# Attention on one Trainium2 core: the four weighted-sum rows of a head pair in one run behind the last transposes

## The chip, the cores and the metric

The kernel runs on one core of one Trainium2 chip. The metric is the device time of one execution in microseconds (us); the host only lays data out before the launch. The kernel is written by hand on top of a scheduler that decides the order of instructions where the code does not pin it; TensorE (PE) does matmuls and transposes, VectorE (DVE) and ScalarE (ACT) do elementwise work, GpSimd (POOL) and SyncE (SP) issue the DMAs here.

## The reference

The model is a two-layer trunk over 512 positions of width 1024. Layer 0 mixes positions with stick-breaking attention, layer 1 with a state-space layer; each is followed by a gated feed-forward block. The change is in layer 0's attention, of which this is the core (16 heads of 64, four blocks of 128 query positions):

```python
z = jnp.einsum('bhqd,bhkd->bhqk', q_blk, kf) * scale
mask = key_pos[None, :] < q_pos[:, None]
log_beta = jax.nn.log_sigmoid(z)
log_1mb = jnp.where(mask, jax.nn.log_sigmoid(-z), 0.0)
suffix = lax.cumsum(log_1mb, axis=3, reverse=True) - log_1mb
w = jnp.where(mask, jnp.exp(log_beta + suffix), 0.0)
o = jnp.einsum('bhqk,bhkd->bhqd', w, vf)
```

The weight of a key is its beta times the product of (1 - beta) over the keys between it and the query. That product telescopes: with R the running product of (1 - beta) from the right, the weight is a difference of two neighbouring values of R, so the kernel multiplies R by differences of V rows and needs no exponentials.

## The kernel before, in words

Heads are worked in eight pairs (pr = 0 to 7; h2 is the head in the pair). For a pair there are, in this order:

- **Projections** (`proj`): q and k of both heads as 128x512 tiles. Numbers are split in a high and a low part, so each product is three matmuls (`mm3`, lines L171, L174, L175). 8 products make k, then 8 make q. ACT and DVE evict them (L770 to L774).
- **Scores** (`z_row`, L782): row i of four, 128 queries against the first (i+1)*128 keys (at least 256), four matmuls (L792, L793). ACT makes `om = sigmoid(-z)` (L797), DVE runs a multiplying scan over it from the right (L798). The om tiles are full 128x512 tiles from one pool of nine (`OMB`).
- **Transposes** (`t_grp`, L803): group 0 turns column block 0 of the four rows, group 1 block 1 of three rows, group 2 blocks 2 and 3; so 8, 6 and 6 transposes for the two heads (L810). ACT evicts each head's group to a `wT` tile (L813), from a pool of four (`NWT`).
- **Weighted sums** (`av`, L818): for row j of the transposed weights and each head, one matmul of 64 output columns (L826) that adds into the pair's `o` bank: 512, 384, 256 and 128 columns for j = 0 to 3. The two heads use the two halves of the array. ACT evicts the sum (L832, or L828 and L829 for pairs 6 and 7).

The order on PE is written by hand (`tc.keep_in_program_order`, here `pe_pin`). `middle(pr)` (L864) serves pairs 1 to 6: it puts the projections of pair pr+1 in pieces between the scores of pair pr and the transposes and sums of pair pr-1. In `follow` order, ACT's and DVE's instructions stay in the written order as well. Into DVE's queue it also puts the `work` steps: up to four multiplications per pair of a weight row block `wg` with the conditioning vector (L198), whose 512 KB are loaded by a DMA that POOL issues (L197) into one of two buffers. `window(7)` and `window(8)` (L836) do the same for the last pairs, with products of the output projection `wo` as the filling; behind them `out_proj` ends the attention.

PSUM has eight banks: six in the pool `mm` and two in `aux`. Row tiles of the scores go to the one or the other (`ZM`), transposes to `mm`, and for pair 7 to `aux` (`TAUX`).

Before the change, `middle` has the sums of rows 0 and 1 ahead of transpose group 2, and the sums of rows 2 and 3 ahead of the scores of row 3.

Of the kernel before, what the change touches and what calls it, by code (L numbers as in the profile page):

```python
# [7 lines left out]
F32 = mybir.dt.float32  # L8
# [3 lines left out]
AF = mybir.ActivationFunctionType  # L12
ALU = mybir.AluOpType
# [3 lines left out]
P = 128  # L17
T = 512
# [40 lines left out]
NU = 4  # L59
NPRE = 3  # L60
KPRE = 5
NWT = 4
MIDN = 2
TAIL = 3
QK = 'kq'
BGA = 3
ZM = ((1, 0), (1, 1), (3, 0), (3, 1))
OMB = 9
TAUX = 7

_COLS = [("c0", KD), ("norm_mix", 2 * KD), ("norm_ffn", 2 * KD), ("b_mod", 96), ("norm_out", KD),
# [18 lines left out]
def _trunk(ctx, tc, I, out, tap):  # L90
    nc = tc.nc
    V, S, G, PE, SP = nc.vector, nc.scalar, nc.gpsimd, nc.tensor, nc.sync
# [13 lines left out]
    def bank(p=None, name="ps"):  # L106
        p = p or mm
        return p.tile([P, 512], F32, tag="b", name=name)
# [22 lines left out]
    maskb = cp.tile([P, T], BF16, tag="maskb", name="maskb")  # L131
# [5 lines left out]
    pin = {"head": []}  # L137
# [112 lines left out]
    def pe_pin(ins):  # L250
        tc.keep_in_program_order(ins)
# [290 lines left out]
    def attention(acc):  # L542
        with ExitStack() as av_, ExitStack() as ac:
# [168 lines left out]
            ap = ac.enter_context(tc.tile_pool(name="attn", bufs=1, reuse_waits="tile"))  # L712
# [20 lines left out]
            scale = HD ** -0.5  # L733
# [12 lines left out]
            def proj(pr, todo=None):  # L746
                units, r = [], [None, None]
                qk[pr] = r
                order = free if todo is None else follow

                def unit(s, w, ps, k):
                    mm3(ps, wk(w, k), (h[0][k], h[1][k]), k == 0, k == KD - 1, pr > 0)
                    if k == KD - 1:
                        if todo is None:
                            evict(s, ps)
                        else:
                            todo.append(lambda: evict(s, ps))

                def evict(s, ps):

                    lo, hi = slice(0, HD), slice(HD, P)
                    if s:
                        kl = kz[pr % 2]
                        st = [ap.tile([P, T], F32R, tag=g, bufs=2, name=f"{g}{pr}") for g in ("kA", "kB")]
                    else:
                        st = [np_.tile([P, T], F32, tag=g, bufs=2, name=f"q_{g}{pr}").bitcast(F32R) for g in ("sq", "nt1")]

                    heads = ((st[0], lo, hi), (st[1], hi, lo))
                    for t, own, other in heads:
                        order("S", lambda: S.activation(t[own], ps[own], AF.Copy))  # L770
                        if s:
                            order("S", lambda: S.activation(t[other], ps[own], AF.Copy))
                    for h2, (t, own, other) in enumerate(heads):
                        order("V", lambda: V.tensor_tensor(kl[h2][own] if s else t[other], ps[own], t[own].bitcast(F32), ALU.subtract))  # L774
                    r[s] = st + kl if s else st

                for nm in QK:
                    s, w, ps = "qk".index(nm), qkw[pr, nm], bank(name=f"{nm}{pr}")
                    units += [lambda s=s, w=w, ps=ps, k=k: unit(s, w, ps, k) for k in range(KD)]
                return units  # L780

            def z_row(pr, i, order=free):  # L782
                qs, ks = qk[pr]
                if i == 0:
                    wts[pr] = [[None] * 4 for _ in range(2)]
                n = (i + 1) * P
                m = max(n, 2 * P)
                zs = []
                for h2 in range(2):
                    z = bank(mm if (i, h2) in ZM else aux, f"z{pr}_{i}_{h2}")  # L790
                    q = qs[h2][:, i * P:(i + 1) * P]
                    pe_pin(PE.matmul(z[:, :m], q, ks[h2][:, :m], start=True, stop=False))  # L792
                    pe_pin(PE.matmul(z[:, :m], q, ks[2 + h2][:, :m], start=False, stop=True))  # L793
                    zs.append(z)
                for h2 in range(2):
                    om = ap.tile([P, T], F32, tag="om", bufs=OMB, name="om")
                    order("S", lambda: S.activation(om[:, :n], zs[h2][:, :n], AF.Sigmoid, scale=-scale))  # L797
                    pin["scan"] = order("V", lambda: V.tensor_tensor_scan(om[:, :n][:, ::-1], om[:, :n][:, ::-1], maskb[:, T - n:][:, ::-1], 1.0, ALU.mult, ALU.max))  # L798
                    wts[pr][h2][i] = om

            wT = {}
# [1 line left out]
            def t_grp(pr, gi, order=free):  # L803
                js = ((0,), (1,), (2, 3))[gi]
                for h2 in range(2):
                    pt = bank(aux if pr >= TAUX else mm, name=f"t{pr}_{h2}_{gi}")
                    c = 0
                    for j in js:
                        for i in range(j, 4):
                            pe_pin(PE.transpose(pt[:, c:c + P], wts[pr][h2][i][:, j * P:(j + 1) * P], ident))  # L810
                            c += P
                    t = ap.tile([P, T], F32, tag="wT", bufs=NWT, name="wT")
                    order("S", lambda: S.activation(t[:, :c], pt[:, :c], AF.Identity, bias=ones[:, 0:1], scale=-1.0))  # L813
                    wT[pr, h2, gi] = t
# [3 lines left out]
            def av(pr, js, order=free):  # L818
                if 0 in js:
                    po[pr] = bank(name=f"o{pr}")  # L820
                for j in js:
                    for h2 in range(2):
                        src = wT[pr, h2, min(j, 2)]
                        src = src[:, 256:384] if j == 3 else src[:, :T - j * P]
                        hd = (2 * pr + h2) * HD
                        pe_pin(PE.matmul(po[pr][h2 * HD:(h2 + 1) * HD, j * P:], vn[:, j, hd:hd + HD], src, start=j == 0, stop=j == 3))  # L826
                if 3 in js and pr >= 6:
                    S.activation(oh[pr], po[pr], AF.Copy)  # L828
                    V.tensor_tensor(ol[pr], po[pr], oh[pr].bitcast(F32), ALU.subtract)  # L829
                elif 3 in js:  # L830
                    o = otile(pr, f"oT{pr}")
                    order("S", lambda: S.activation(o, po[pr], AF.Copy))  # L832
                    tap(f"o{pr}", o)
                    oT[pr] = o

            def window(pr, units, fill=FILL, hooks={}):  # L836
                n, done = len(units), 0
                pv = pr - 1
                for st, share in enumerate(fill):
                    want = -(-n * share // 16)  # L840
                    for u in units[done:want]:
                        u()
                    done = max(done, want)
                    if pv >= 0:
                        if st == TST[0]:
                            t_grp(pv, 0)
                            t_grp(pv, 1)
                        if st == TST[1]:
                            av(pv, (0, 1))
                            t_grp(pv, 2)  # L850
                        if st == TST[2]:
                            av(pv, (2, 3))
                    if pr < 8 and st < 4:
                        z_row(pr, st)
                    if st in hooks:
                        hooks[st]()
                for u in units[done:]:
                    u()
# [5 lines left out]
            def middle(pr, gemvs, split, own=lambda k: None):  # L864
                todo, pv = [], pr - 1
                units = proj(pr + 1, todo)
                work = lambda q: bg(gemvs[q], lined=True, queue=G)

                def run(a, b):
                    for u in units[a:b]:  # L870
                        u()

                run(0, 7)
                work(0)
                split[0]()
                work(1)
                t_grp(pv, 0, follow)
                t_grp(pv, 1, follow)
                z_row(pr, 0, follow)
                run(7, 8)  # L880
                z_row(pr, 1, follow)
                work(2)
                todo[0]()
                split[1]()
                run(8, 13)
                own(0)
                av(pv, (0, 1), follow)
                t_grp(pv, 2, follow)
                z_row(pr, 2, follow)
                own(1)  # L890
                run(13, 16)
                todo[1]()
                av(pv, (2, 3), follow)
                z_row(pr, 3, follow)
                for k in range(2, KPRE):
                    own(k)
# [742 lines left out]
```

## Time and profile before

| what | value |
|---|---|
| time, median of 3 runs | 1176.8 us (1173.6 to 1178.79) |
| span of the profiled execution | 1174.0 us |
| PE busy | 1158.9 us, 99% |
| DVE busy | 857.7 us, 73% |
| ACT busy | 563.5 us, 48% |
| attention's weighted sums on PE | first at 101.0 us, last at 237.7 us of the span |

The span runs from the first to the last instruction of one profiled execution; no time of its own is given for that execution beside its span. It is 2.8 us under the median of the three timed runs, and inside their spread. In the profile a matmul's end is modelled and matmuls overlap, so what a piece of PE work costs is read from the starts of rows that follow each other, not from the second column of a row. A row of the timeline gives start, length, engine, line, operation, the tiles written and read, shape and count; a bracket gives idle time ahead of it and what ended it.

### The profile page before, as it was taken

Reading aid. Unit: us, or ns where it says so; the run is one execution under the profiler, and the core shown is the slowest. Engines: PE = TensorE matmul, PEld = TensorE weight load, DVE = VectorE, ACT = ScalarE, POOL = GpSimd, SP = SyncE. Lnnn points to the kernel's source line nnn. Section 1 sums busy time; section 2 is a strip of 40 time slices with the busy share of each in tenths; the row PEclk is TensorE's granted clock in tenths of the full one; section 3 lists DMA queues with packets and bytes.
Section 4 is the critical chain, followed back from the end, with each engine's and each line's share of the span. In section 5 each row is a group of like instructions: output and inputs, shape, how many; then the busy total and the mean of one; then the engine's idle time right before and its main releaser. Section 6 shows DMA issues by size and latency. Waiting matters only on the chain.

```text
span 1174.0 us, 16592 instructions
## 1 busy us (share of the span) xinstructions
PE 1158.9 (99%) x6242; PEld 964.2 (82%) x6242; DVE 857.7 (73%) x1311; ACT 563.5 (48%) x896; POOL 270.8 (23%) x278
## 2 busy tenths in 40 slices
PE   8999999999999999999999999999999999999997
PEld 7887777699788888888889888789888888888887
DVE  6968888775998666787757599887598378744555
ACT  6756667456453244413346477647443144422443
POOL 2001110000298799979800000000000000000003
PEclk8999999999999999999999999999999999999999
DMA  8873656331267858797756598671176357432322
GB/s 320 292 264 116 192 162 195 111 123 55 78 189 268 247 167 252 198 292 253 230 151 223 149 353 293 207 255 50 49 231 217 107 153 184 133 123 73 92 69 72
DMA packets 91618, 211.01 MB, mean 180 GB/s; under 512 B 19601, under 2 KB 37905, under 8 KB 91538
## 3 DMA queue, kind: packets, MB, share of 16 engines
q1 hardware_dynamic: 78562, 191.08, 51.0%
q0 software_dynamic: 4656, 16.78, 4.5%
q10 hardware_dynamic: 8320, 2.10, 0.8%
q8 instruction: 49, 0.80, 0.3%
q14 instruction: 31, 0.25, 0.1%
HBM read 188.68 MB, written 21.24 MB: 179 GB/s over the span
## 4 chain that ended last, share of the span: by engine, by line
PE 78%; DVE 7%; issue 7%; DMA 5%; ACT 2%; POOL 1%; SPq 1%; POOLq 0%; DVEq 0%; ACTq 0%
PE up L171 13%; PE up L174 13%; PE up L175 13%; PE dn L171 6%; PE dn L174 6%; PE dn L175 6%; DMA wg<-in_w_modT_dram 3%; PE u L174 1%; PE u L171 1%; PE u L175 1%; PE wo L171 1%; PE wos L174 1%; PE wo L175 1%; PE wo L174 1%; PE wos L175 1%
## 5 line engine op out<-in xcount | busy, mean ns | idle before, releaser
L171 PE MATMUL up<-hH,up_h 128*128 128x512 f32 x640 | 249.7, 391 | 0.3 <-DVE ca L461 0.3
L175 PE MATMUL up<-hH,up_l 128*128 128x512 f32 x640 | 249.3, 390 | 0.3 <-DVE up_l L166 0.3
L174 PE MATMUL up<-hL,up_h 128*128 128x512 f32 x640 | 249.3, 390 | 0.0
L461 DVE SCALAR_TENSOR_TENSOR ca<-up,small,ca 128x511 f32<-128x511 f32 (+1 forms) x176 | 131.6, 748 | 120.7 <-ACT ca L459 117.6
L171 PE MATMUL dn<-gH,dn_h 128*128 128x512 f32 (+1 forms) x394 | 145.0, 369 | 0.0
L198 DVE SCALAR_TENSOR_TENSOR wg<-wg,cact 128x1024 f32<-128x1024 f32 x96 | 121.4, 1281 | 31.7 <-DMA wg<-in_w_modT_dram 31.6
L174 PE MATMUL dn<-gL,dn_h 128*128 128x512 f32 (+1 forms) x394 | 144.5, 367 | 0.0
L175 PE MATMUL dn<-gH,dn_l 128*128 128x512 f32 (+1 forms) x394 | 144.4, 366 | 0.0
L171 PEld LDWEIGHTS up<-hH,up_h 128*128 128x128 f32 x640 | 120.1, 188 | 26.5 <-issue 1.5
L175 PEld LDWEIGHTS up<-hH,up_l 128*128 128x128 f32 x640 | 120.1, 188 | 25.9 <-DVE up_l L166 1.1
L174 PEld LDWEIGHTS up<-hL,up_h 128*128 128x128 f32 x640 | 120.1, 188 | 24.4
L459 ACT ACTIVATE ca<-up,small 128x512 f32<-128x512 f32 x88 | 68.2, 775 | 149.5 <-PE up L175 149.5
L1511 POOL TENSOR_SCALAR xa<-x,Anorm_out 128x256 f32<-128x256 f32 x7 | 5.7, 818 | 570.3 <-DVE x L355 570.3
L165 ACT ACTIVATE up_h<-up_r 128x1024 fp32r<-128x1024 f32 x80 | 84.2, 1052 | 75.3 <-PE dn L174 58.1
L166 DVE TENSOR_TENSOR up_l<-up_r,up_h 128x1024 fp32r<-128x1024 f32 x80 | 116.3, 1454 | 5.4 <-ACT up_h L165 4.5
L355 DVE SCALAR_TENSOR_TENSOR x<-dn,mod,x 128x512 f32<-128x512 f32 (+1 forms) x55 | 37.4, 680 | 71.4 <-PE dn L175 71.4
L171 PEld LDWEIGHTS dn<-gH,dn_h 128*128 128x128 f32 x394 | 74.3, 189 | 12.9 <-issue 0.6
L174 PEld LDWEIGHTS dn<-gL,dn_h 128*128 128x128 f32 x394 | 74.3, 189 | 12.1
L175 PEld LDWEIGHTS dn<-gH,dn_l 128*128 128x128 f32 x394 | 74.3, 189 | 12.1
L165 ACT ACTIVATE dn_h<-dn_r 128x1024 fp32r<-128x1024 f32 (+1 forms) x48 | 46.7, 982 | 46.2 <-PE dn L174 38.5
L166 DVE TENSOR_TENSOR dn_l<-dn_r,dn_h 128x1024 fp32r<-128x1024 f32 (+1 forms) x48 | 61.6, 1283 | 0.8 <-ACT dn_h L165 0.5
L477 ACT ACTIVATE gH<-gm 128x512 fp32r<-128x512 f32 x44 | 27.1, 616 | 67.3 <-DVE gm L473 67.3
(349 smaller groups left out, 2311.0 us busy)
## 6 DMA issues: line engine op xcount, KB each, us to landing
up_r<-in_w_up_dram SPq DMA_DIRECT2D x80, 512.0 KB
wg<-in_w_modT_dram SPq DMA_DIRECT2D x71, 512.0 KB
dn_r<-in_w_down_dram SPq DMA_DIRECT2D x32, 512.0 KB
wg<-in_w_modT_dram POOLq DMA_DIRECT2D x25, 512.0 KB, 4.0
wgs<-in_w_modT_dram SPq DMA_DIRECT2D x16, 512.0 KB
dn_r<-in_w_down_dram SPq DMA_DIRECT2D x16, 384.0 KB
wv_r<-in_w_v_dram SPq DMA_DIRECT2D x8, 512.0 KB
wk_r<-in_w_qk_dram SPq DMA_DIRECT2D x8, 512.0 KB
```

Of the source, the lines that this page charges most:

```text
L165: order("S", lambda: S.activation(wh[:, :n], raw[:, :n], AF.Copy))
L166: pin["split"] = order("V", lambda: V.tensor_tensor(wl[:, :n], raw[:, :n], wh[:, :n].bitcast(F32), ALU.subtract))
L171: ins = PE.matmul(ps, ah, bh, start=start, stop=False)
L174: PE.matmul(ps, ah, bl, start=False, stop=False)
L175: PE.matmul(ps, al, bh, start=False, stop=stop)
L198: mul = lambda: V.scalar_tensor_tensor(w, w, 1.0, cact, ALU.mult, ALU.mult, accum_out=raw[:, col:col + 1])
L355: add = lambda: V.scalar_tensor_tensor(xs, pv, gate, xs, ALU.mult, ALU.add)
L459: follow("S", lambda: S.activation(ca, ps, AF.Identity, bias=small[:, cb:cb + 1], scale=tapw[2]))
L461: follow("V", lambda: V.scalar_tensor_tensor(ca[:, q:], ps[:, :T - q], tapw[2 - q], ca[:, q:], ALU.mult, ALU.add))
L477: follow("S", lambda: S.activation(gh, m, AF.Copy))
L1511: G.tensor_scalar(xa[k], x[k][:, cb], a[:, k:k + 1], 0.0, ALU.mult, ALU.add)
```

## The change

The sums of rows 0 and 1 no longer stand ahead of transpose group 2. All four rows of sums are asked for in one call where rows 2 and 3 stood, ahead of the scores of row 3. Since the sums of a pair now read six transposed tiles at once, the pool of `wT` tiles has six buffers for four. The om tiles get the width of their row (128 to 512) and two buffers for each row, in place of nine full-width ones.

```diff
-NWT = 4
+NWT = 6
...
-OMB = 9
...
                 for h2 in range(2):
-                    om = ap.tile([P, T], F32, tag="om", bufs=OMB, name="om")
-                    order("S", lambda: S.activation(om[:, :n], zs[h2][:, :n], AF.Sigmoid, scale=-scale))
-                    pin["scan"] = order("V", lambda: V.tensor_tensor_scan(om[:, :n][:, ::-1], om[:, :n][:, ::-1], maskb[:, T - n:][:, ::-1], 1.0, ALU.mult, ALU.max))
+                    om = ap.tile([P, n], F32, tag=f"om{i}", bufs=2, name="om")
+                    order("S", lambda: S.activation(om, zs[h2][:, :n], AF.Sigmoid, scale=-scale))
+                    pin["scan"] = order("V", lambda: V.tensor_tensor_scan(om[:, ::-1], om[:, ::-1], maskb[:, T - n:][:, ::-1], 1.0, ALU.mult, ALU.max))
                     wts[pr][h2][i] = om
...
# window
                         if st == TST[1]:
-                            av(pv, (0, 1))
                             t_grp(pv, 2)
                         if st == TST[2]:
-                            av(pv, (2, 3))
+                            av(pv, range(4))
...
# middle
                 own(0)
-                av(pv, (0, 1), follow)
                 t_grp(pv, 2, follow)
                 z_row(pr, 2, follow)
                 own(1)
                 run(13, 16)
                 todo[1]()
-                av(pv, (2, 3), follow)
+                av(pv, range(4), follow)
                 z_row(pr, 3, follow)
```

Lines of the changed kernel are one lower than before (L826 is L825). In the order, PE in `middle(3)` before: behind a product of q for pair 4 stand the four sums of rows 0 and 1 of pair 2 (`o2`), then its transpose group 2 (`t2_0_2`, `t2_1_2`) and the scores of row 2 of pair 3 (`z3_2`):

```order
L175 MATMUL q4_1243<-hH4_230,wq4_l_1161 128x512
L826 MATMUL o2_1365<-wT_1285,vn_601 64x512
L826 MATMUL o2_1365<-wT_1292,vn_601 64x512
L826 MATMUL o2_1365<-wT_1298,vn_601 64x384
L826 MATMUL o2_1365<-wT_1304,vn_601 64x384
L810 MATMUL t2_0_2_1370<-consts_87,om_1203 128x128
L810 MATMUL t2_0_2_1370<-consts_87,om_1236 128x128 x2
L810 MATMUL t2_1_2_1376<-consts_87,om_1206 128x128
L810 MATMUL t2_1_2_1376<-consts_87,om_1239 128x128 x2
L792 MATMUL z3_2_0_1382<-kA3_1151,q_sq3_1218 128x384
```

The same place of the changed kernel: transpose group 2 follows the product of q at once.

```order
L174 MATMUL q4_1243<-hH4_230,wq4_l_1161 128x512
L809 MATMUL t2_0_2_1365<-consts_87,om_1198 128x128
L809 MATMUL t2_0_2_1365<-consts_87,om_1236 128x128 x2
L809 MATMUL t2_1_2_1371<-consts_87,om_1201 128x128
L809 MATMUL t2_1_2_1371<-consts_87,om_1239 128x128 x2
L791 MATMUL z3_2_0_1377<-kA3_1151,q_sq3_1213 128x384
```

And nine matmuls of q later (the rows above of before have them behind `z3_2` as well), the changed kernel has all eight sums of pair 2 in one run, ahead of the scores of row 3 (`z3_3`), where before only the last four stood:

```order
L174 MATMUL q4_1243<-hH7_233,wq4_l_1161 128x512
L825 MATMUL o2_1404<-wT_1285,vn_601 64x512
L825 MATMUL o2_1404<-wT_1292,vn_601 64x512
L825 MATMUL o2_1404<-wT_1298,vn_601 64x384
L825 MATMUL o2_1404<-wT_1304,vn_601 64x384
L825 MATMUL o2_1404<-wT_1369,vn_601 64x256
L825 MATMUL o2_1404<-wT_1375,vn_601 64x256
L825 MATMUL o2_1404<-wT_1369,vn_601 64x128
L825 MATMUL o2_1404<-wT_1375,vn_601 64x128
L791 MATMUL z3_3_0_1415<-kA3_1151,q_sq3_1213 128x512
```

The other place is `window(8)`, the last pair, on PE. Before, its sums (`o7`) stand in three places between products of the output projection (`wo`); the second of them, and transpose group 2 behind it:

```order
L171 MATMUL wo3_2295<-oH3_2002,wo3_h_2172 128x512
L174 MATMUL wo3_2295<-oL3_2003,wo3_h_2172 128x512
L826 MATMUL o7_2238<-wT_2214,vn_601 64x384
L826 MATMUL o7_2238<-wT_2220,vn_601 64x384
L810 MATMUL t7_0_2_2243<-consts_87,om_2126 128x128
L810 MATMUL t7_0_2_2243<-consts_87,om_2153 128x128 x2
L810 MATMUL t7_1_2_2249<-consts_87,om_2129 128x128
L810 MATMUL t7_1_2_2249<-consts_87,om_2156 128x128 x2
L171 MATMUL wo2_2022<-oH6_2010,wo2_h_1908 128x512
```

The changed kernel has group 2 six matmuls behind the other transposes of pair 7 (`t7_1_1`), and the sums of rows 0 and 1 in one run behind it; the sums of rows 2 and 3 follow twelve matmuls of `wo` later, so there are two places instead of three.

```order
L174 MATMUL wo1_2018<-oH6_2010,wo1_l_1903 128x512
L809 MATMUL t7_0_2_2238<-consts_87,om_2121 128x128
L809 MATMUL t7_0_2_2238<-consts_87,om_2153 128x128 x2
L809 MATMUL t7_1_2_2244<-consts_87,om_2124 128x128
L809 MATMUL t7_1_2_2244<-consts_87,om_2156 128x128 x2
L170 MATMUL wo2_2022<-oH6_2010,wo2_h_1908 128x512
L173 MATMUL wo2_2022<-oL6_2011,wo2_h_1908 128x512
L174 MATMUL wo2_2022<-oH6_2010,wo2_l_1909 128x512
L825 MATMUL o7_2263<-wT_2201,vn_601 64x512
L825 MATMUL o7_2263<-wT_2208,vn_601 64x512
L825 MATMUL o7_2263<-wT_2214,vn_601 64x384
L825 MATMUL o7_2263<-wT_2220,vn_601 64x384
```

DVE's, ACT's, POOL's and SP's instructions keep their order in the attention, except that one or two short vectors of the modulation move by a few places on DVE in three pairs. Behind the attention a few residual and split steps at its end trade places.

## The prediction

> **What bounds the kernel now.** I read the page first, then the busy times of the attention in stretches of 20 us, then the waits there, the chain of waits, and last the timelines of PE and DVE.
>
> ```profile
> PE 1158.9 (99%) x6242; PEld 964.2 (82%) x6242; DVE 857.7 (73%) x1311; ACT 563.5 (48%) x896; POOL 270.8 (23%) x278
> ```
>
> ```profile
> 120.00:140.00 20.00, 20.00 (x108) 14.62 (x104) 17.69 (x29) 11.98 (x24) 2.64 (x5) 1.00 0.61 186
> 200.00:220.00 20.00, 19.03 (x103) 13.57 (x97) 16.13 (x22) 11.32 (x23) 0.00 (x0) 1.00 0.32 111
> ```
>
> By these lines (PE, PEld, DVE, ACT, POOL, granted clock, DMA share, GB/s) PE never rests from 120 to 140 us and rests 0.97 us from 200 to 220, always at the full clock. A change that takes PE work out would then shorten the kernel one to one. But DVE is at 17.69 of 20 us as well, and a full PE may still be one that has only just not waited. The waits from 78 to 245 us (waiting group, releaser, sum, times, longest) say what DVE's missing time is:
>
> ```profile
> DVE wg L198 <- DMA wg<-in_w_modT_dram: 19.0, 12, 3.1
> ...
> DVE oL L829 <- ACT oH L828: 4.8, 2, 3.6
> ...
> PEld t L810 <- DVE om L798: 1.4, 3, 0.7
> ```
>
> DVE waits there for the modulation rows that POOL loads, 19.0 us in 12 waits; its next wait in the list, 4.8 us, is for the eviction of the last two pairs' sums (L829). In the middle pairs it waits for neither PE nor ACT. DVE's timeline shows the loop:
>
> ```profile
> 147.97 2.34 DVE L798 TENSOR_TENSOR_SCAN om<-om,maskb 128x512 f32<-128x512 f32 x2
> 150.23 1.20 DVE L198 SCALAR_TENSOR_TENSOR wg<-wg,cact 128x1024 f32<-128x1024 f32 x1
> ...
> 155.75 1.23 DVE L198 SCALAR_TENSOR_TENSOR wg<-wg,cact 128x1024 f32<-128x1024 f32 x1 [2.02 <-DMA wg<-in_w_modT_dram]
> ...
> 159.76 1.22 DVE L198 SCALAR_TENSOR_TENSOR wg<-wg,cact 128x1024 f32<-128x1024 f32 x1 [0.88 <-DMA wg<-in_w_modT_dram]
> ...
> 163.59 1.80 DVE L798 TENSOR_TENSOR_SCAN om<-om,maskb 128x384 f32<-128x384 f32 x2
> ...
> 166.82 2.34 DVE L798 TENSOR_TENSOR_SCAN om<-om,maskb 128x512 f32<-128x512 f32 x2
> ```
>
> The scans of row 3 are followed by a multiplication that frees a `wg` buffer; that lets POOL issue the next load, DVE waits for it (2.02 us), for the one behind it (0.88), and then works without a pause to the next pair's scans of row 3. From scan to scan that is 166.82 - 147.97 = 18.85 us. PE's round, from one pair's first sums to the next pair's, is 138.36 - 119.78 = 18.58 us:
>
> ```profile
> 119.46 0.39 PE L175 MATMUL q<-hH,wq_l 128*128 128x512 f32 x1
> 119.78 1.73 PE L826 MATMUL o<-wT,vn 128*64 128x512 f32 x8
> 121.43 0.88 PE L810 MATMUL t<-consts,om 128*128 128x128 f32 x6
> 122.06 0.42 PE L792 MATMUL z<-kA,q_sq 128*128 128x384 f32 x1
> ...
> 122.85 0.40 PE L171 MATMUL q<-hH,wq_h 128*128 128x512 f32 x1
> ...
> 124.70 0.39 PE L175 MATMUL q<-hH,wq_l 128*128 128x512 f32 x1
> 125.02 0.87 PE L826 MATMUL o<-wT,vn 128*64 128x256 f32 x8
> 125.82 0.51 PE L792 MATMUL z<-kA,q_sq 128*128 128x512 f32 x1
> ...
> 126.87 0.40 PE L171 MATMUL k<-hH,wk_h 128*128 128x512 f32 x1
> ...
> 131.44 0.39 PE L175 MATMUL k<-hH,wk_l 128*128 128x512 f32 x1
> 131.67 1.69 PE L810 MATMUL t<-consts,om 128*128 128x128 f32 x14
> 133.11 0.36 PE L792 MATMUL z<-kA,q_sq 128*128 128x256 f32 x1
> ...
> 133.67 0.40 PE L171 MATMUL k<-hH,wk_h 128*128 128x512 f32 x1
> ...
> 138.36 1.72 PE L826 MATMUL o<-wT,vn 128*64 128x512 f32 x8
> ```
>
> So DVE's round is 0.27 us longer than PE's, though PE looks full. PE had a lead to lose, and at the end of `middle(6)` it is lost; PE's timeline and the chain that ended last agree:
>
> ```profile
> 201.89 0.50 PE L174 MATMUL wo<-oL,wo_h 128*128 128x512 f32 x1 [0.27 <-DVE oL L930]
> ...
> 206.87 0.66 PE L810 MATMUL t<-consts,om 128*128 128x128 f32 x4 [0.24 <-DVE om L798]
> 207.98 0.98 PE L810 MATMUL t<-consts,om 128*128 128x128 f32 x7 [0.46 <-DVE om L798]
> ```
>
> ```profile
> 206.73 1.21 DVE om L798
> 207.98 0.98 PE t L810 x7
> ```
>
> The three waits come to 0.97 us. The chain runs over DVE, POOL and the loads up to 207.98 us and over PE from there. Before that point, PE work that is saved turns into longer waits at these places; behind it, it counts.
>
> **The change part by part.** *No instruction is added or taken out.* The same 16 sums a pair (two passes of eight), 20 transposes and scores stand on PE; DVE, ACT, POOL and SP do what they did. What changes is how often PE goes over from products to sums and back.
>
> *Middle pairs and window(7).* Before, two stretches hold the sums. From the last product ahead of rows 0 and 1 to the first product behind the scores of row 2: 122.85 - 119.46 = 3.39 us. Around rows 2 and 3: 126.87 - 124.70 = 2.17 us. Together 5.56 us. After the change the first stretch is a product, six transposes and four scores. The rows around 131.67 show such a stretch with 14 transposes and narrower scores, 133.67 - 131.44 = 2.23 us. Of it I take off eight transposes at (133.11 - 131.67) / 14 = 0.10, which is 0.82, and add (122.85 - 122.06) - (133.67 - 133.11) = 0.23 for the wider scores: 1.64 us. The second stretch becomes 2.17 us and the sums of rows 0 and 1 inside a run. Alone they take 121.43 - 119.78 = 1.65 us up to the next operation, with the way out of the sums in it. For that way out I have these rows of the last pair:
>
> ```profile
> 226.43 0.39 PE L174 MATMUL wo<-oL,wo_h 128*128 128x512 f32 x1
> 226.66 0.40 PE L175 MATMUL wo<-oH,wo_l 128*128 128x512 f32 x1
> 226.99 1.08 PE L826 MATMUL o<-wT,vn 128*64 128x512 f32 x4
> 228.00 0.50 PE L171 MATMUL wo<-oH,wo_h 128*128 128x512 f32 x1
> 228.34 0.40 PE L174 MATMUL wo<-oL,wo_h 128*128 128x512 f32 x1
> ```
>
> Product to product is 0.23 us. Product to sums is 226.99 - 226.66 = 0.33, so the way in costs 0.10. The first product behind sums takes 228.34 - 228.00 = 0.34, so the way out costs 0.11. Inside a run rows 0 and 1 cost about 1.65 - 0.10 = 1.55 us, and the two stretches 1.64 + 2.17 + 1.55 = 5.36 us: 0.20 us saved a pair, one way in and one way out. If the way out is already in the next operation and not in the 1.65 us, it is 0.10; if the transposes behind sums are slowed as well, up to 0.30. I take 0.20, the value both workings give.
>
> [...]
>
> Six pairs (`middle(1)` to `middle(6)`) lie ahead of 207.98 us: 6 x 0.20 = 1.2 us that PE will wait for DVE instead, counted at 0. `window(7)` lies behind it and counts: 0.20.
>
> *window(8).* Three places of sums become two, and transposes come directly behind a product, which costs nothing extra (131.67 - 131.44 = 0.23). One way in and one way out less: 0.20 us, bounds 0.10 and 0.30. The transposes of group 2 now follow group 1 closely and use the same two banks, so they wait for ACT's evictions:
>
> ```profile
> 223.80 2.55 ACT L813 ACTIVATE wT<-t,ones 128x512 f32<-128x512 f32 x4 [1.89 <-PE t L810]
> ```
>
> These four end at 226.35; the six products between take PE to 226.66 + 0.23 = 226.89. That is 0.5 us to spare, so I cost it at nothing; ACT a whole eviction late (2.55 / 4 = 0.64) would make it 0.1 us. The pair's last sums come some microseconds earlier; PE had `wo` products to fill that time, so nothing is won.
>
> *Buffers.* Six `wT` tiles are what one run of eight sums reads; the next pair's first transposes come 5.85 us behind the run (131.67 against 125.82), so their buffers are free. The row-sized om tiles add a wait of the row 3 sigmoids for the previous pair's scans of row 3, a round earlier, and ahead of the weight split queued behind them on ACT: free at once. Both at 0.
>
> The sum is 0.20 + 0.20 = 0.4 us (0.2 to 0.6): the span of 1174.0 becomes 1173.6, and the median of the runs, 2.8 us above the span, 1176.8 - 0.4 = **1176.4 us**.
>
> **The rivals.** *PE bounds the whole attention.* For it speaks PE's 20.00 of 20 us; against it the DVE round and the three waits. Then all eight pairs pay: 8 x 0.20 = 1.6 us, 1175.2 us, and with the upper price 8 x 0.30 = 2.4, 1174.4.
>
> *The run of sums loses its side-by-side heads (slower).* The two heads of a row share the array:
>
> ```profile
> L826 PE MATMUL o<-wT,vn x128: 272/458/643, 101.0 to 237.7; 128*64 128x512 f32 x32, 128*64 128x384 f32 x32, 128*64 128x256 f32 x32, 128*64 128x128 f32 x32
> ```
>
> Records of up to 643 ns, eight of them done in 1.65 us. If a longer run, whose second half waits for ACT head by head, made them go singly, a pair's 1.55 + 0.80 = 2.35 us of sums would double; 8 x 2.35 = 19 us, 1195.6 less what DVE still hides (0.27 a round): some 1194. It decides as soon as a head has to wait; today's first runs also wait for ACT inside, and still pair.
>
> *Nothing is left.* The last two stretches lean on DVE too: `window(8)` follows the scans of its own row 3. Then 1176.8 us.
>
> **How the numbers follow.** A change of 0.5%, 5.9 us, is about what a measurement of this kernel can tell. The forecast has 0.62, the PE rival 0.20, no gain 0.12, the slower rival 0.03; 0.03 are left for a gain that I don't see. All but the last two lie within 0.5%; with spread, faster 0.04, same 0.92, slower 0.04. The three runs spread over 5.2 us, so either end gets 2.6: up from 1176.8 to 1179.4, down from the PE rival's 1174.4 to 1171.8, say 1172.0.
>
> **What would show it.** In the changed profile, the first stretch (product, transposes, scores) should last about 1.64 us and the run of eight about 3.7 with its scores; PE's waits for DVE between 200 and 208 us should grow from 0.97 to about 2 us; the transposes that end the last of them should again start near 208 us, and the first transposes of `window(8)` should follow them 0.1 to 0.3 us sooner than before. I am wrong if those transposes start over 1 us earlier (PE bound), if DVE's round changes, or if the sums last longer than 2.5 us a pair.

## The result, and the profile after

| kernel | median | runs | ratio to before (95%) | profiled span |
|---|---|---|---|---|
| before | 1176.57 us (1173.6 to 1179.75) | 20 | | 1174.0 us |
| after | 1179.26 us (1176.51 to 1181.9) | 20 | 1.0023 (1.0015 to 1.0032) | 1176.1 us |

The changed kernel is 2.7 us slower. That is within 0.5%, and inside the stated range, but the forecast was 0.4 us to the other side, and the interval leaves out both a gain and no change. The time lies inside the range only because the range was widened by the spread of the three runs: none of the rivals leads there.

First the part that came as foretold: PE's timeline of the changed kernel in a middle pair (the lines of the changed kernel are one lower than before's at the sums and the transposes).

```profile
136.21 0.40 PE L174 MATMUL q<-hH,wq_l 128*128 128x512 f32 x1
136.44 0.82 PE L809 MATMUL t<-consts,om 128*128 128x128 f32 x6
137.02 0.42 PE L791 MATMUL z<-kA,q_sq 128*128 128x384 f32 x1
...
137.80 0.39 PE L170 MATMUL q<-hH,wq_h 128*128 128x512 f32 x1
...
139.65 0.40 PE L174 MATMUL q<-hH,wq_l 128*128 128x512 f32 x1
139.98 2.38 PE L825 MATMUL o<-wT,vn 128*64 128x512 f32 x16
142.28 0.50 PE L791 MATMUL z<-kA,q_sq 128*128 128x512 f32 x1
...
143.32 0.39 PE L170 MATMUL k<-hH,wk_h 128*128 128x512 f32 x1
...
158.25 2.37 PE L825 MATMUL o<-wT,vn 128*64 128x512 f32 x16
```

The stretch with six transposes lasts 137.80 - 136.21 = 1.59 us (forecast 1.64), the run of sums with its scores 143.32 - 139.65 = 3.67 us (3.72). Together 5.26 us, where the two stretches took 5.56 us before: 0.30 us saved a pair, the upper bound that was given and not the 0.20 taken. The round is 158.25 - 139.98 = 18.27 us, 0.31 less than the 18.58 of before. The heads still share the array: the 16 sums, with records of up to 644 ns, take 142.28 - 139.98 = 2.30 us up to the scores.

Where the time went is seen in the start of a few steps, each counted from the first product of V in its own profile (21.36 us before, 20.17 after) and compared with before:

| changed kernel minus before | us |
|---|---|
| last product of q of pair 7 | -3.36 |
| first scores of row 0 in window(7) | +2.85 |
| first scores of row 3 in window(7) | +2.54 |
| first product of the FFN | +2.16 |

The FFN is the feed-forward block behind the attention. The profiled spans themselves differ by 2.1 us: these 2.16, 1.19 less ahead of V and 1.12 more behind the FFN's first product. That last part runs from 910.25 to 913.57 us over the profiles of all the kernels here, whose code behind the attention is the same, so its 1.12 us say nothing about the change.

In this execution PE arrives early. Of the 3.36 us, 1.51 is only work that has moved behind this point: the sums took 2.31 us there against 0.80. The other 1.85 is the six pairs' saving, 6 x 0.31. Then, between the end of `middle(6)` and `window(7)`, 6.2 us are lost, and the two windows win back 0.31 and 0.38. PE's timeline of the changed kernel at that place:

```profile
199.82 0.50 PE L173 MATMUL wo<-oL,wo_h 128*128 128x512 f32 x1 [1.26 <-DVE oL L927]
...
200.86 0.40 PE L174 MATMUL wo<-oH,wo_l 128*128 128x512 f32 x1
203.62 0.77 PE L170 MATMUL wo<-oH,wo_h 128*128 128x512 f32 x1 [2.36 <-DVE q_nt L773]
204.18 0.63 PE L173 MATMUL wo<-oL,wo_h 128*128 128x512 f32 x1
204.61 0.63 PE L174 MATMUL wo<-oH,wo_l 128*128 128x512 f32 x1
...
208.70 1.93 PE L809 MATMUL t<-consts,om 128*128 128x128 f32 x14
210.38 0.37 PE L791 MATMUL z<-kA,q_sq 128*128 128x256 f32 x1
```

And the same twelve products, transposes and scores of before:

```profile
203.14 0.39 PE L171 MATMUL wo<-oH,wo_h 128*128 128x512 f32 x1
...
206.13 0.49 PE L810 MATMUL t<-consts,om 128*128 128x128 f32 x3
...
208.72 0.36 PE L792 MATMUL z<-kA,q_sq 128*128 128x256 f32 x1
```

Two things are new. The first matmul of the third output tile waits 2.36 us for `q_nt`, which is no operand of it. And the products behind that wait stand 0.43 us apart instead of 0.23. The sum closes: the moved sums 1.51, the waits 1.26 + 2.36 - 0.97 = 2.65, the twelve products (208.70 - 203.62) - (206.13 - 203.14) = 2.09; together 6.25, beside the 6.20 us found. The forecast's wait for `om` at the transposes is gone: all 14 start at 208.70 us, and nothing holds them; before, the last of them were let go at 207.98.

The stretches of the changed kernel (the last columns are granted clock, DMA share, GB/s) show the slow products as a halved clock (0.51); before's clock is 1.00 there, in the second fence.

```profile
200.00:203.60 3.60, 1.26 (x5) 0.70 (x6) 3.54 (x6) 3.06 (x5) 0.00 (x0) 0.73 0.61 245
203.60:208.60 5.00, 4.98 (x12) 3.94 (x13) 5.00 (x6) 0.00 (x0) 0.00 (x0) 0.51 0.01 3
208.60:212.00 3.40, 3.38 (x25) 2.88 (x24) 2.16 (x4) 2.54 (x6) 0.00 (x0) 1.00 0.59 186
```

```profile
203.00:208.00 5.00, 4.30 (x22) 2.92 (x20) 4.92 (x7) 3.92 (x6) 0.00 (x0) 1.00 0.29 107
```

Between 203.6 and 208.6 us PE reads 4.98 of 5.00 us busy, though the twelve products there lost 2.09 us; of these columns and rows only the clock (0.51) and the distance of the starts (0.43 us) show it.

DVE's timeline of the changed kernel says why `q_nt` was late:

```profile
195.39 0.68 DVE L773 TENSOR_TENSOR kz<-k,kA 64x512 fp32r<-64x512 f32 x1
196.08 0.69 DVE L773 TENSOR_TENSOR kz<-k,kB 64x512 fp32r<-64x512 f32 x1
196.81 2.36 DVE L165 TENSOR_TENSOR wo_l<-wo_r,wo_h 128x1024 fp32r<-128x1024 f32 x2
199.09 0.68 DVE L927 TENSOR_TENSOR oL<-oT,oH 128x512 fp32r<-128x512 f32 x1
199.69 1.80 DVE L797 TENSOR_TENSOR_SCAN om<-om,maskb 128x384 f32<-128x384 f32 x2
201.41 0.66 DVE L927 TENSOR_TENSOR oL<-oT,oH 128x512 fp32r<-128x512 f32 x1
202.08 0.68 DVE L773 TENSOR_TENSOR q_sq<-q,q_sq 64x512 fp32r<-64x512 f32 x1
202.78 0.69 DVE L773 TENSOR_TENSOR q_nt<-q,q_nt 64x512 fp32r<-64x512 f32 x1
203.50 2.34 DVE L797 TENSOR_TENSOR_SCAN om<-om,maskb 128x512 f32<-128x512 f32 x2
```

DVE never pauses in these rows. `q_sq` and `q_nt` read pair 7's q tile in PSUM; PE had ended it at 194.9 us, and DVE's second reading of it is over at 203.47, behind two splits of k, two of `wo`, two of `oL` and two scans. The third `wo` tile needs one of the six banks of `mm`, and in the changed program it has got the bank of that q tile. In the order of the two built programs this is one row. Before, `wo2`'s first matmul waits for ACT; in the changed kernel for DVE:

```
L171 MATMUL wo2_2022<-oH0_1928,wo2_h_1908 128x512 [waits Activation_49]
L170 MATMUL wo2_2022<-oH0_1928,wo2_h_1908 128x512 [waits DVE_49,PE_49]
```

Before, its bank was that of `o5`, the sums of pair 5, which ACT's copy of them frees (the built programs give `wo2` and `o5` one bank before, `wo2` and pair 7's q one bank in the changed kernel). No edit of the diff names a `wo` tile. The program's order decides which bank is handed out next; that the sums now end later against q's evictions, so that q's bank counts as the older one, is the likely reason, but it is argued and not shown.

Two theories were set against each other. **The bank:** PE is held by the third `wo` tile's bank, and with another bank the loss goes. **The arrival:** PE simply arrives some 2 us too early at a place where DVE is late; it idles there whatever it waits for, the clock falls, and the loss stays.

### The profile page after: what moved, and what is told of

Read it like the earlier page. It is cut to its first block, busy times and chain, and to the rows that moved or that the text cites. A ratio compares the mean times of both kernels' runs of the same rounds, so it can differ in the third digit from the quotient of the medians.

```text
span 1176.1 us, 16597 instructions
## 1 busy us (share of the span) xinstructions
PE 1156.7 (98%) x6242; PEld 964.3 (82%) x6242; DVE 858.0 (73%) x1311; ACT 564.1 (48%) x896; POOL 272.5 (23%) x278
## 4 chain that ended last, share of the span: by engine, by line
PE 67%; POOL 9%; issue 8%; DVE 7%; DMA 6%; ACT 2%; SPq 0%; POOLq 0%; DVEq 0%; ACTq 0%
PE up L170 11%; PE up L173 11%; PE up L174 11%; PE dn L170 5%; PE dn L173 5%; PE dn L174 5%; DMA wg<-in_w_modT_dram 2%; PE wo L170 1%; PE wo L173 1%; PE u L173 1%; PE wo L174 1%; PE u L170 1%; PE u L174 1%; PE wos L173 1%; PE wos L174 1%
## 5 line engine op out<-in xcount | busy, mean ns | idle before, releaser
L165 DVE TENSOR_TENSOR up_l<-up_r,up_h 128x1024 fp32r<-128x1024 f32 x80 | 113.4, 1417 | 10.3 <-ACT up_h L164 9.3
```

The lines of the kernel that those rows point to most:

```text
L165: pin["split"] = order("V", lambda: V.tensor_tensor(wl[:, :n], raw[:, :n], wh[:, :n].bitcast(F32), ALU.subtract))
```

## The experiments

**The changed kernel with `wo2` on `o5`'s bank,** as before had it. One line:

```diff
-                    part[mt][1] = bank(name=f"wo{mt}")
+                    part[mt][1] = po[5] if mt == 2 else bank(name=f"wo{mt}")
```

> The changed kernel, with the third output-projection bank (wo2) put on the bank of the last sums o5 instead of q7's. Bank theory: the loss comes from wo2 waiting for DVE to read q7 (2.36 us) and the half clock that follows; then this wait is gone, the granted clock stays at 1.00 from 200 to 209 us, and the time is 0.4 to 1.6 us below before (ratio 0.9986 to 0.9997). Arrival theory: PE comes early and must idle for DVE somewhere in any case, the clock falls all the same, and the ratio stays at 1.002 to 1.003. Downstream theory (the loss arises behind the attention): ratio also stays at 1.002, though the clock is full.

Measured: 1175.39 us (12 runs), ratio 0.9991 (0.9976 to 1.0005). In its profile PE still comes 3.2 us early, and the wait for `q_nt` is gone. PE's timeline (this kernel's `wo2` carries the name `o`):

```profile
200.46 0.50 PE L173 MATMUL wo<-oL,wo_h 128*128 128x512 f32 x1 [1.84 <-DVE oL L927]
...
206.06 1.93 PE L809 MATMUL t<-consts,om 128*128 128x128 f32 x14
```

```profile
200.00:203.00 3.00, 2.54 (x8) 2.08 (x9) 2.97 (x5) 1.55 (x3) 0.00 (x0) 0.76 0.81 289
203.00:206.00 3.00, 3.00 (x10) 2.32 (x10) 2.96 (x4) 1.58 (x2) 0.00 (x0) 0.68 0.10 41
```

One wait of 1.84 us for `oL` is left, and in this execution the clock fell even behind that one (0.76 and 0.68 in the two stretches), where a full clock had been expected. Yet the time is back at before's or a little under it. This profile and the changed kernel's come to the last product of q within 0.14 us of each other, and to the first scores of `window(7)` 2.56 us apart. The bank's theory holds; the arrival's falls, and so does the third one, that the loss arises behind the attention.

**The same kernel once more,** on another chip, to narrow the interval (no edit against the one above).

> The changed kernel with wo2 on o5's bank, once more, to narrow the interval: bank theory 0.9986 to 0.9997, arrival theory 1.002 to 1.003.

Measured: 1176.78 us (11 runs), ratio 1.0000 (0.9989 to 1.0011). Its waits there are 1.92 us for `oL`, 0.25 and 0.46 us for `om`, and the clock is 1.00. PE comes 1.87 us early in this execution, hardly more than the 1.51 of moved work. The expected 0.9986 to 0.9997 was met by the first of the two measurements and missed by the second, whose interval still reaches into it. By both, the change without its bank is neither faster nor slower than before by anything that can be measured.

**Before with the bank of pair 7's q given to `wo2`,** and nothing else:

```diff
+                    qps[pr, nm] = ps
...
-                    part[mt][1] = bank(name=f"wo{mt}")
+                    part[mt][1] = qps[7, "q"] if mt == 2 else bank(name=f"wo{mt}")
```

> The kernel before, with nothing changed but that wo2 is put on q7's bank. Bank theory: wo2 waits about 2 us for DVE's second read of q7, the clock falls to one half behind it, and the kernel is 1.5 to 3.5 us slower than before (ratio 1.001 to 1.003), though its sums stand where they stood. Arrival theory: PE is not early here, DVE's reads are nearly done, the clock stays full, ratio 0.9995 to 1.0008. Downstream theory: 1.000.

Measured: 1179.89 us (12 runs), ratio 1.0028 (1.0013 to 1.0042): the whole loss, with the old order of sums. PE's timeline (here `wo2` carries the name `q`):

```profile
206.34 0.50 PE L171 MATMUL q<-oH,wo_h 128*128 128x512 f32 x1 [2.28 <-DVE q_nt L776]
...
209.22 1.92 PE L813 MATMUL t<-consts,om 128*128 128x128 f32 x14
```

It swallows the old waits for `om` as well, so the scores behind it are 1.43 us later than before's, less than the wait itself. The clock stayed at 1.00 (the products are 0.23 us apart), where half had been expected. The profiled execution, 1177.09 us, was the fastest of the twelve, so it shows 1.4 of the 3.3 us; what the others lost beside that is not seen. By the times the bank alone is enough, early arrival or not.

**The changed kernel with the old places of the sums in `middle(6)` only:**

```diff
+                if pr == 6:
+                    av(pv, (0, 1), follow)
                 t_grp(pv, 2, follow)
...
-                av(pv, range(4), follow)
+                av(pv, (2, 3) if pr == 6 else range(4), follow)
```

> The changed kernel with the sums of middle(6) alone put back in two places; wo2 then stands on o5's bank by itself. Bank theory: no wait for q7, full clock, ratio 0.9988 to 1.0000. Arrival theory: PE is still over 1 us early after five joined pairs, so it idles and the clock falls, ratio 1.001 to 1.003. Downstream theory: ratio 1.002.

Measured: 1175.77 us (12 runs), ratio 0.9989 (0.9973 to 1.0004). Nothing in it names a bank, but `wo2` is back on `o5`'s, and the old waits are back with it; PE's timeline:

```profile
202.40 0.50 PE L173 MATMUL wo<-oL,wo_h 128*128 128x512 f32 x1 [0.43 <-DVE oL L929]
...
207.38 0.66 PE L809 MATMUL t<-consts,om 128*128 128x128 f32 x4 [0.24 <-DVE om L797]
208.50 0.99 PE L809 MATMUL t<-consts,om 128*128 128x128 f32 x7 [0.46 <-DVE om L797]
```

It is the order in `middle(6)`, just ahead of the first `wo` tiles, that turned the bank over.

**The changed kernel, its wait filled with work.** Is it the halved clock that costs? Three matmuls with zeros stand ahead of `wo2`, so that PE does not rest:

```diff
+                    if mt == 2:
+                        for q in range(NDUM):
+                            pe_pin(PE.matmul(part[1][1], zeros, x[q], start=False, stop=False))
                     part[mt][1] = bank(name=f"wo{mt}")
```

> The changed kernel with three 128x512 matmuls by zeros into wo1's bank (they add nothing) ahead of wo2's first product, so that PE works during its wait for q7. If the half clock is the larger part of the loss, the granted clock stays at 1.00 behind the wait, the 12 products behind it run at 0.23 us instead of 0.43, and the time falls by 1.5 to 2.5 us against the changed kernel (ratio to before 1.000 to 1.001). If the wait itself is the loss, the ratio stays at 1.002.

Measured: 1178.32 us (12 runs), ratio 1.0023 (1.0005 to 1.0041), where 1.000 to 1.001 had been expected if the halved clock was the larger part: the filling did not give the time back. In the profile, of the fastest of these runs (1174.94 us), the clock does stay up (the row counts six records for the three matmuls):

```profile
202.37 2.74 PE L948 MATMUL wo<-x,zeros 128*128 128x512 f32 x6
204.90 0.47 PE L173 MATMUL wo<-oH,wo_h 128*128 128x512 f32 x1
```

```profile
203.00:209.00 6.00, 6.00 (x28) 4.00 (x26) 5.94 (x9) 2.50 (x5) 0.00 (x0) 1.00 0.12 49
```

and the scores of `window(7)` are 1.50 us later than before's instead of 2.85. The 1.35 us between the two are less than the 2.09 that the slow products cost, and the two executions differ in more than the clock: DVE is done with q 0.90 us later in this one (184.20 us behind the first product of V, against 183.30). So in the changed kernel's profile a good part of the 2.85 us goes with the clock. By time the split stays open: the interval holds all of the loss and a fifth of it.

**The buffers alone:** six `wT` buffers and om tiles by row, with the sums in their old places in `middle` and `window`.

```diff
+                            av(pv, (0, 1))
                             t_grp(pv, 2)
...
-                            av(pv, range(4))
+                            av(pv, (2, 3))
...
+                av(pv, (0, 1), follow)
                 t_grp(pv, 2, follow)
...
-                av(pv, range(4), follow)
+                av(pv, (2, 3), follow)
```

> The buffers of the change alone: six wT tiles and the row-sized om tiles, with all sums in their old places; wo2 stands on o5's bank as before. Bank theory: nothing waits that did not, clock as before, ratio 0.999 to 1.001. Buffer theory (the row-sized tiles or their new waits of the sigmoids cost the time): ratio 1.002 or more.

Measured: 1177.52 us (10 runs), ratio 1.0012 (0.9999 to 1.0024). Its waits near 200 us are 1.14 us for `oL`, 0.22 and 0.46 us for `om`, none for `q_nt`: the buffers did not move `wo2` off its bank. Whether they cost something (at most 2.8 us by the interval) is not settled. One profile is no measure of 1 or 2 us here: counted as in the table above, the first product of the FFN comes 2.39 us later than before's in this one, and 1.66 us earlier in that of the kernel with `middle(6)` put back. So the cause rests on the times of the kernels that only move the bank, and not on the table.

**The joined sums in the windows alone** (of the diff above the last five lines, those in `middle`; `window` is left as changed).

> The changed kernel with the sums of all six middle pairs back in two places, joined in window(7) and window(8) alone; wo2 on o5's bank. The step of the forecast that joined sums save 0.2 us for each pair behind the last wait for DVE: from the first scores of window(7) to the first product of the feed-forward the stretch is 0.4 to 0.7 us shorter than before, and the ratio is 0.999 to 1.000. If the loss were in the windows: ratio 1.002.

Measured: 1175.84 us (10 runs), ratio 1.0003 (0.9991 to 1.0015); too little for the time to tell. In its profile the stretch from the first scores of `window(7)` to the FFN is 0.68 us shorter than before's (53.19 against 53.87): 0.31 in `window(7)`, 0.37 behind it. These two savings are there, as foretold, and are larger than the 0.20 + 0.20 taken.

**Less work for DVE.** If DVE's lateness is what makes the six pairs' lead worthless, a lighter DVE must let it through. The two kernels leave out a part of the modulation: in the middle pairs the modulation's multiplications take 256 of 1024 columns, once in before and once in the changed kernel with `wo2` on `o5`'s bank:

```diff
-        mul = lambda: V.scalar_tensor_tensor(w, w, 1.0, cact, ALU.mult, ALU.mult, accum_out=raw[:, col:col + 1])
+        ww, ca_ = (w[:, :256], cact[:, :256]) if lined and queue is G else (w, cact)
+        mul = lambda: V.scalar_tensor_tensor(ww, ww, 1.0, ca_, ALU.mult, ALU.mult, accum_out=raw[:, col:col + 1])
```

> The kernel before, with the modulation multiplications that stand in the middle pairs cut to a quarter of their columns (part of the modulation is left out; the loads stay), so that DVE has some 3 us less work a pair. If DVE's round bounds these pairs, PE's waits for oL and om between 200 and 209 us (0.97 us) go and the time falls by about 1 us, ratio 0.999. If PE bounds them, the same waits would be gone as well, but the control for the next kernel is what counts.

> The changed kernel with wo2 on o5's bank and the same lighter multiplications (the same part left out). If joined sums shorten PE's rounds and only DVE's round kept that from counting, the whole lead of seven to eight pairs, about 0.3 us each, now counts: 2 to 2.5 us less than the light kernel before, ratio to the kernel before 0.996 to 0.998. If DVE's round was not what absorbed the lead, it is equal to the light kernel before within 0.7 us.

Measured: before so lightened 1174.41 us (10 runs), ratio 0.9988 (0.9969 to 1.0007); the changed kernel so lightened 1171.47 us (4 runs), ratio 0.9962 (0.9947 to 0.9977). PE does not wait for DVE from 190 to 209 us in either. Now the change is worth 2.9 us between the two medians, near the 2.6 that the traces give (6 x 0.31 and 0.31 + 0.38); in the two profiles the first product of the FFN comes 2.74 us apart. The time has only four runs behind it, and the two intervals overlap by 0.0008.

**The same with nothing left out:** three of the four multiplications that `middle(6)` puts into DVE's queue go behind `window(7)`.

```diff
-            middle(6, (2, 1, 1), [lambda: out_w(0), out_w2], o_split)
+            middle(6, (1, 0, 0), [lambda: out_w(0), out_w2], o_split)
...
-                bg(4, False)
+                bg(7, False)
```

> The changed kernel with wo2 on o5's bank, and with three of the four modulation steps of middle(6) moved behind window(7), where DVE idles; the result is whole. If DVE's round absorbs PE's lead of 3.2 us at the end of middle(6), at least 1 us of that lead is kept and the time is 1.5 to 3 us below before (ratio 0.9975 to 0.999). If the lead is lost to the clock or to a later load instead, ratio 0.9991 as without the move.

> The kernel before with the same three steps moved, as the control: its 0.97 us of waits for DVE between 200 and 209 us go, and no lead is there to be kept, so 0.5 to 1 us below before (ratio 0.9992 to 0.9997). If it gains as much as the changed kernel with the move, the joined sums have no part in it.

Measured: the changed kernel with `o5`'s bank and this move 1173.79 us (12 runs), ratio 0.9978 (0.9966 to 0.9991), faster than before by an interval that leaves out no change; before with this move 1176.14 us (11 runs), ratio 0.9996 (0.9983 to 1.0009). The stretches of the first of the two:

```profile
190.00:200.00 10.00, 10.00 (x57) 7.50 (x55) 8.66 (x13) 9.59 (x20) 0.00 (x0) 1.00 0.56 173
200.00:220.00 20.00, 19.99 (x112) 15.56 (x109) 13.89 (x19) 12.31 (x24) 0.00 (x0) 1.00 0.21 72
```

PE rests 0.01 us in 30 at the full clock, where before rested 0.97. The move without the joined sums gives nothing to be measured, nor do the joined sums without the move; the two together give 2.6 us by the ratio (1.1 to 4.0). With the move, the joined sums make 2.3 us between the means of the 12 and the 11 runs (0.8 to 3.6 when the runs are drawn again and again as independent ones), though the two intervals against before overlap by 0.0008.

That the six pairs' lead is what is kept, the profile does not show. In it PE waits four times for DVE's scans inside the middle pairs (0.20 to 0.44 us each), and its last product of q comes only 1.16 us earlier than before's, less than the 1.51 of moved sums. What is gone are the waits near 200 us. Against the control's profile the first scores of `window(7)` come 0.6 us earlier and the first product of the FFN 1.6 us; the larger part of that lies in the two windows.

## Why the prediction was wrong

**The step that failed** is the first of the change part by part: "No instruction is added or taken out", and "What changes is how often PE goes over from products to sums and back". It takes every wait of the tiles behind the moved sums to stay as it was, and so puts a change of their banks at nothing without a reason; banks were looked at only for the transposes of pair 7. But where an order decides which bank a pool hands out, a moved run of sums can change the bank of a later tile. Here it was the third `wo` tile's, with a new wait of 2.36 us on DVE's queue. Giving it the old bank took the loss away (0.9991 and 1.0000), giving before the new one brought it (1.0028). The step on the buffers, "Both at 0", is not the one that turned the bank: with the buffers alone `wo2` stays on `o5`'s. The two rows with the waits of `wo2` stand in the order of the built programs, so the new wait could have been seen ahead of the run, though not its length.

**What the lead is worth.** "PE work that is saved turns into longer waits" and is "counted at 0": with the old bank no gain can be measured (0.9991, 1.0000 and 0.9989, each with an interval that holds 1). But PE resting can be more than lost time here: in two profiled executions the clock fell to half (0.50) behind such waits, and that was no rival of the forecast. In one of the two, with `o5`'s bank, the halved clock cost nothing that the time shows: its transposes, at 206.06 us, are not held for `om` any more.

**The DVE round was read from one round.** The forecast set 18.85 us of DVE against PE's 18.58. DVE's scans of row 3 in before, and in the changed kernel:

```profile
111.39 2.34 DVE L798 TENSOR_TENSOR_SCAN om<-om,maskb 128x512 f32<-128x512 f32 x2
129.03 2.34 DVE L798 TENSOR_TENSOR_SCAN om<-om,maskb 128x512 f32<-128x512 f32 x2
...
184.46 2.34 DVE L798 TENSOR_TENSOR_SCAN om<-om,maskb 128x512 f32<-128x512 f32 x2
205.59 2.34 DVE L798 TENSOR_TENSOR_SCAN om<-om,maskb 128x512 f32<-128x512 f32 x2
```

```profile
109.90 2.34 DVE L797 TENSOR_TENSOR_SCAN om<-om,maskb 128x512 f32<-128x512 f32 x2
...
183.00 2.34 DVE L797 TENSOR_TENSOR_SCAN om<-om,maskb 128x512 f32<-128x512 f32 x2
203.50 2.34 DVE L797 TENSOR_TENSOR_SCAN om<-om,maskb 128x512 f32<-128x512 f32 x2
```

Before's first round is 17.64 us, and four rounds take 73.07, 18.27 each; the changed kernel's take 73.10. A round is long or short by one or two waits for a load: in before, 17.64 us with one of 1.81 us, 18.85 us with two of 2.02 and 0.88 us. So in these two profiles DVE was not slower than PE's 18.58 us over four pairs; it falls behind in the last round, of 21.13 us, in which the `wo` splits and the `oL` stand. In other executions it is slower. In the second measurement of the kernel with `o5`'s bank four of DVE's rounds take 74.54 us, 18.64 each, and PE waits for the scans inside the middle pairs:

```profile
131.85 0.98 PE L809 MATMUL t<-consts,om 128*128 128x128 f32 x7 [0.20 <-DVE om L797]
150.63 0.98 PE L809 MATMUL t<-consts,om 128*128 128x128 f32 x7 [0.29 <-DVE om L797]
```

There the saving of the joined sums is lost pair by pair, and not only at the end of `middle(6)`. The conclusion, that DVE decides near 208 us, agrees with the lighter kernels, in which PE does not wait for DVE and the change pays.

**The saving was undersized:** 0.31 us a pair in the middle and in `window(7)`, 0.38 behind it, against 0.20; the bound of 0.30 was the better value. The two behind the last wait for DVE come to 0.7 us.

**The rivals.** PE did not bound the whole attention (its 1175.2 needs the lead to count; that came only with a lighter DVE). The heads kept sharing the array (16 sums in 2.30 us). The forecast and "Nothing is left" lie 0.4 us apart, less than the intervals of the kernels with `o5`'s bank tell. The signs named for the forecast came in part. 1.64 and 3.7 us came as 1.59 and 3.67. The waits near 200 us grew from 0.97 to 3.62 us instead of 2; with `o5`'s bank they were 1.84 and 2.63 us. That they grow is no sign of the joined sums, though: the kernel with the sums of all middle pairs in their old places waits 1.66 us for `oL`, 0.23 and 0.46 us for `om`, 2.35 in all. The transposes started at 208.70 us, but with no wait ahead of them, and the first ones of `window(8)` followed the first scores of `window(7)` 0.34 us sooner than before (14.11 against 14.45), just above the 0.1 to 0.3 named.

**Left open:** how the 2.7 us divide between the wait and the halved clock, whether the buffers cost anything, and how much of the gain with the moved multiplications is the six pairs' lead.

## What to carry to other kernels

Before an edit that moves work is costed at nothing, list the waits of the tiles *behind* it in the built order: a pool's next bank is part of the order, and a tile that gets the bank of a value with a slow second reader has that reader's whole queue ahead of it. Where PE has a lead that another engine takes away, look for the edit that lightens that engine at the place where they meet; here neither of the two gave a gain that could be measured alone. Read a loop's round from several rounds and more than one execution, and look at the clock column before a busy stretch is called a full one.

## What the runs showed of the hardware

The halved clock was not expected. In the changed kernel the products stand 0.43 us apart from 204.18 to 208.45 us, where before's stand 0.23 us apart, behind waits of 1.26 and 2.36 us within 5 us; with `o5`'s bank a half-clock stretch came behind a wait of 1.84 us. The rows of the changed kernel and of the kernel with `o5`'s bank:

```profile
201.70:208.40 6.70, 4.78 (x11) 3.80 (x12) 6.64 (x9) 1.54 (x2) 0.00 (x0) 0.50 0.11 42
```

```profile
201.55:204.90 3.35, 3.35 (x10) 2.59 (x9) 3.27 (x5) 1.58 (x3) 0.00 (x0) 0.50 0.45 169
```

The clock is 1.00 up to 201.6 and from 208.5 us on in the first, up to 201.5 and from 205.0 us on in the second, so the two stretches last about 6.8 and 3.4 us. In the second PE goes on working at 200.46 us, and the clock falls about 1 us later. But a wait of 1.92 us, in the second measurement of the same kernel, and one of 2.28 us, in before with q's bank, left the clock at 1.00. So in these executions the length of one wait does not decide it (behind 1.84 us the clock fell, behind 1.92 and 2.28 us it did not), and two executions alike in their order can differ in it.

The mean granted clock of a whole execution does not show where it was lost. In before and in the changed kernel:

```profile
0.00:20.00 20.00, 16.33 (x76) 13.87 (x76) 10.10 (x22) 11.01 (x20) 5.99 (x15) 0.83 0.90 331
```

```profile
200.00:220.00 20.00, 17.62 (x80) 13.65 (x82) 14.26 (x19) 8.08 (x17) 0.00 (x0) 0.83 0.27 97
```

Before loses clock in its first 20 us and is at 1.00 from there to 1160 us; the changed kernel is at 1.00 up to 200 us. Over the timed runs the mean is 0.9958 in before (89 runs) and 0.9940 in the changed kernel (20), but that difference can't be put down to the place near 200 us.
